# Weight-block sums and sums of squares as accumulating transfers, and one bank copy moved to ScalarE, in a two-layer streaming encoder

## The chip, the cores and the metric

The kernel runs on one core of a Trainium2 chip. The metric is the device time of one execution in microseconds (us); of several runs the median counts. Nothing else runs on the core, and all inputs and outputs lie in device memory.

## What is computed

Two trunk layers work on 656 tokens: 16 meta tokens and 512 prompt tokens of one new stream, and 8 running streams of 16 tokens. Cut to what matters here:

```python
def swiglu(x, w_gate, w_up, w_down):
    return (silu(x @ w_gate) * (x @ w_up)) @ w_down       # 1024 -> 2816 -> 1024

def trunk_layer(x, ...):
    h = x + 0.5 * swiglu(rmsnorm(x, n1), f1g, f1u, f1d)
    ...                                                    # mixers: pooling, short convolution, attention
    h = h + mixed @ w_out
    h = h + 0.5 * swiglu(rmsnorm(h, n2), f2g, f2u, f2d)
```

All data is float32. Four feed-forward networks (FFNs), two per layer, take most of the time.

## The kernel before

Activations lie with channels on the 128 partitions and tokens along the free dimension. Every product splits both operands into a high and a low part and takes three matmuls (`mm3`), so a weight block of 128 channels needs a rounded copy (ScalarE, `act`, L120) and the remainder (VectorE, a subtraction, `tt`, L134) before TensorE can use it. Such a prepared piece of four blocks is a **slab**; raw weights are loaded by the SP queue (L333), and `prep_next` makes slabs of them in order, one after each group of matmuls (`pump`).

The gate and up projections of an FFN work by **pairs** of 128 output columns. A pair is a 2x2 block product done with seven block products instead of eight (`run_pair`): weights a11, a12, a21, a22 (each 128x512, that is 256 KB) become the seven slabs a11, a12, a21', a11', a12', s3, a22, where

- s3 = a11 + a21 (first sum),
- a21' = a21 + a22 (second), a11' = a11 + a21' (third), a12' = a12 + a11' (fourth).

The four sums are made in place by GpSimd in `sums` (L394); each reads what the one before wrote, or overwrites what it read. The raw weights of a pair lie in two tiles A1 (a11, a12) and A2 (a21, a22). There are two sets of such tiles, called raw and rawb in the profile, which pairs use in turn; the s3 buffers (in the tile Wa) are two as well. A set can be loaded again when its last slab is prepared.

TensorE runs a pair as seven groups of 12 matmuls (`seven`, L143) of 128x328 each, into three PSUM banks. In the program's order they are B11, B21, Q1, Q2, B22, T3, and T4, which is held back (`late`) into the next pair. B11, Q2, T3 and T4 add up in one bank b1 (tag mm), so b1 must be read out between two of them: after T3, VectorE reads it (`s[3]` = b1 + p5, L134) before T4 may write.

An FFN has 20 such pairs, 11 column blocks less the first, each with gate and up. Between them stand four groups of eight down-projection units. So the pairs come in runs: 3 at the start, then 6, 6 and 5 in a row, each followed by eight down units. Pairs of a run are written here as g3, u3 (gate and up of column block 3).

The norms need sums of squares over the eight channel blocks. In `feed` (L528) ScalarE squares each block as it is finished, GpSimd adds it to `acc`, and VectorE adds the eighth. This happens ahead of five of the norms, with six additions by GpSimd in each.

The order of instructions on each engine is set once, when the program is built, by a scheduler that goes by priorities and by its own model of durations; each engine then runs its queue strictly in that order, waiting where an operand is late.

Of the kernel before, what the change touches and what calls it, by code (L numbers as in the profile page):

```python
# [7 lines left out]
AF = mybir.ActivationFunctionType  # L8
ALU = mybir.AluOpType

P = 128
# [45 lines left out]
class Builder:  # L57
# [261 lines left out]
    def load_next(self):  # L319
        u = self.units[self.n_load]  # L320
        if self.n_done < u["after"]:
            return False
        spots = self.take("raw", len(u["src"]), u["ring"] == "F")
        if spots is None:
            return False
        u["raw"] = []
        for at, (k, parts) in zip(spots, u["src"]):
            raw = at
            if raw is None:
                raw = self.rp.tile([P, KD * P], F32, tag="raw", name=self.name("raw"))  # L330
            raw = raw.rearrange("p (k c) -> p k c", k=KD)[:, :k, :]
            for k0, kn, src in parts:
                self.nc.sync.dma_start(raw[:, k0:k0 + kn, :], src.rearrange("(k p) c -> p k c", p=P))  # L333
            u["raw"].append((at, raw))
        self.n_load += 1
        return True

# [53 lines left out]
    def sums(self, u, i):  # L391
        if i == 1:
            (_, A1), (_, A2) = u["raw"]
            add = lambda out, a, b: self.nc.gpsimd.tensor_tensor(out, a, b, op=ALU.add)  # L394
            s3 = self.s3[u["turn"]].rearrange("p (k c) -> p k c", k=4)
            a11, a12, a21, a22 = A1[:, 0:4], A1[:, 4:8], A2[:, 0:4], A2[:, 4:8]
            add(s3, a11, a21)
            add(a21, a21, a22)
            add(a11, a21, a11)
            add(a12, a11, a12)  # L400


    def run_units(self, units):
# [104 lines left out]
    def feed(self, to, l, m, hi):  # L508

        c0, c1 = self.halves[hi]  # L510
        gain = {"mixer": "mix_norm", "ffn1": "ffn1_norm", "ffn2": "ffn2_norm"}[to]
        if to == "mixer":
            self.gained(self.H[:, m, c0:c1], l, m, c0, c1, gain)
        if hi == 0:
            return
        c0 = self.halves[0][0]
        n = c1 - c0
        if to != "mixer":
            self.blocks(l, m, gain, c0, n // 2)
        acc, s = self.acc[:, :n], self.sq[self.fed % 2][:, :n]  # L520
        if self.fed == 0:
            self.act(acc, self.H[:, m, c0:c1], AF.Square)
        else:
            self.act(s, self.H[:, m, c0:c1], AF.Square)
            if self.fed == KD - 1:
                self.tt(acc, acc, s, ALU.add)
            else:
                self.nc.gpsimd.tensor_tensor(acc, acc, s, op=ALU.add)  # L528
        self.fed += 1
        if self.fed == KD:  # L530
            self.fed = 0
            halves = self.halves
            self.pending = lambda: self.scales(to, halves)
# [81 lines left out]
    def pair_unit(self, w, f, run, **kw):  # L615

        c = [slice((f + r) * P, (f + r + 1) * P) for r in range(2)]
        self.turn = not self.turn
        return dict(slabs=[4] * 7, src=[(KD, [(0, KD, w[:, x])]) for x in c], prep=self.prep_pair, then=self.sums,
                    run=self.run_pair, evict=run, ring="F", turn=int(self.turn), **kw)  # L620

    def col_unit(self, w, f, r, run):

# [63 lines left out]
    def run_pair(self, u):  # L687

        c0 = self.halves[0][0]
        n = self.halves[0][1] - c0  # L690
        b1, b2, b3 = self.psum("mm"), self.psum("z"), self.psum("z")
        p5 = self.copies[u["turn"]][:, :n]
        f = self.factor[:, c0:c0 + 2 * n]
        S = self.sil if u["evict"] == self.gate_out else self.up
        S = S[:, :4 * n]
        s = [S[:, i * n:(i + 1) * n] for i in range(4)]
        self.clock += 1
        self.seven(u, b1, B11, n, True)
        self.act(s[0], b1[:, :n], AF.Copy)
        self.pump(1)  # L700
        if self.late:
            self.late()
        self.finish_pending()
        self.seven(u, b3, B21, n, True)
        self.tt(s[0], b3[:, :n], s[0], ALU.add)
        self.pump(1)
        self.seven(u, b2, Q1, n, True)
        self.act(p5, b2[:, :n], AF.Copy)
        self.pump(1)
        self.seven(u, b1, Q2, n, False)  # L710
        self.act(s[1], b1[:, :n], AF.Copy)
        self.pump(1)
        self.seven(u, b2, B22, n, False)
        self.tt(s[1], b2[:, :n], s[1], ALU.add)
        self.mul(S[:, :2 * n], S[:, :2 * n], f)
        u["evict"](u, 0, n)
        self.pump(1)
        self.seven(u, b1, T3, n, False)
        self.tt(s[3], b1[:, :n], p5, ALU.add)
        self.stt(s[3], s[3], -1.0, f[:, n:], ALU.mult, ALU.mult)  # L720
        self.pump(1)

        def last():
            self.late = None
            self.seven(u, b1, T4, n, False)
            self.stt(s[2], b1[:, :n], -1.0, f[:, :n], ALU.mult, ALU.mult)
            u["evict"](u, 1, n)
            self.pump(1)
        self.late = last
        self.slot_tail()  # L730
# [507 lines left out]
    def token_scale(self, hi, sums):  # L1238
        c0, c1 = HALF_ALL[hi]
        self.scale_of(sums, c0, c1, False, self.sil, self.up)  # L1240
# [343 lines left out]
```

## Time and profile before

| what | value |
|---|---|
| median of 3 runs (2888.08 to 2892.82) | 2888.17 us |
| the profiled execution's own time | 2890.04 us |
| its span in the profile | 2888.3 us |
| TensorE busy | 2829.0 us, 98% |
| VectorE busy | 1936.6 us, 67% |
| ScalarE busy | 1289.9 us, 45% |
| GpSimd busy | 598.2 us, 21% |
| transfers | 224.27 MB, mean 78 GB/s |

Engines are named PE (TensorE), DVE (VectorE), ACT (ScalarE), POOL (GpSimd) and SP (SyncE, whose queue SPq issues the loads). A row names the line of the helper that recorded an operation, so tile names tell more than lines: ws and slabs are prepared weights, raw and rawb are raw weights, XR and ra hold split activations, mm and z are PSUM banks, Wa is working memory. In a timeline row stand the start, the duration, the engine, the operation, out<-in, and in brackets how long the engine was idle before and what ended that.

### The profile page before, as it was taken

How to read it: one execution, taken by the hardware profiler on the slowest of the kernel's cores; microseconds unless marked ns; L12 is line 12 of the kernel's file. 1: busy time of each engine (PE TensorE's matmuls, PEld its weight loads, DVE VectorE, ACT ScalarE, POOL GpSimd, SP SyncE). 2: the span in 40 equal slices, each digit the busy share in tenths (PEclk: the TensorE clock that was granted, in tenths of full speed). 3: DMA queues.
4: the chain of work that ended last, by engine and by line, in shares of the span. 5: the costliest groups of instructions: out<-in, count | busy, mean ns of one | idle time of the engine just before them, and what ended most of it. 6: DMA issues, size and time to landing. Idle time of an engine off the chain costs nothing.

```text
span 2888.3 us, 47733 instructions
## 1 busy us (share of the span) xinstructions
PE 2829.0 (98%) x19179; PEld 2781.5 (96%) x19179; DVE 1936.6 (67%) x3262; ACT 1289.9 (45%) x2464; POOL 598.2 (21%) x481
## 2 busy tenths in 40 slices
PE   7999999999999999999999999999999999999999
PEld 6999999999999999999999999999999999999999
DVE  8686675876444877675786675768764458675764
ACT  5343344776323443343443443447763234343433
POOL 2233231011000123132223241311110002232230
PEclk8999999999999999999999999999999999999999
DMA  3222322222222322222312322222222223223222
GB/s 113 81 86 69 88 76 74 79 77 69 66 74 74 88 81 66 82 80 74 88 52 81 88 74 81 83 71 72 75 73 66 79 75 88 76 67 92 81 71 76
DMA packets 437169, 224.27 MB, mean 78 GB/s; under 512 B 10110, under 2 KB 436290, under 8 KB 436946
## 3 DMA queue, kind: packets, MB, share of 16 engines
q1 hardware_dynamic: 436452, 220.90, 26.2%
q8 instruction: 150, 2.46, 0.3%
q14 instruction: 73, 0.60, 0.1%
q10 hardware_dynamic: 494, 0.32, 0.0%
HBM read 212.87 MB, written 8.31 MB: 77 GB/s over the span
## 4 chain that ended last, share of the span: by engine, by line
PE 81%; DVE 10%; POOL 4%; DMA 3%; ACT 1%; issue 1%; ACTq 0%; SPq 0%; POOLq 0%; DVEq 0%
PE z L143 50%; PE mm L143 29%; DVE Wa L134 2%; DMA rawb<-in_ffn_w_up_dram 2%; DVE ws L134 2%; DVE Wa L131 2%; DVE slabs L134 2%; POOL rawb L394 1%; POOL raw L394 1%; DVE XR L134 1%; POOL Wa L394 1%; DMA raw<-in_ffn_w_gate_dram 1%; PE aux L143 1%; ACT ws L120 0%; DVE ra L134 0%
## 5 line engine op out<-in xcount | busy, mean ns | idle before, releaser
L143 PE MATMUL mm<-XR,ws 128*128 128x328 f32 (+3 forms) x4848 | 802.6, 314 | 12.6 <-DVE Wa L134 12.6
L143 PEld LDWEIGHTS mm<-XR,ws 128*128 128x128 f32 x4848 | 738.0, 188 | 20.4 <-DVE Wa L134 16.0
L143 PE MATMUL z<-XR,ws 128*128 128x328 f32 (+3 forms) x3924 | 629.2, 313 | 13.5 <-ACT XR L120 6.5
L143 PEld LDWEIGHTS z<-XR,ws 128*128 128x128 f32 x3924 | 597.1, 189 | 15.3 <-ACT XR L120 6.8
L134 DVE TENSOR_TENSOR ws<-raw,ws 128x512 fp32r<-128x512 f32 (+1 forms) x429 | 311.2, 728 | 175.8 <-ACT ws L120 174.0
L143 PE MATMUL z<-ra,ws 128*128 128x328 f32 (+1 forms) x2688 | 421.0, 312 | 0.2
L120 ACT ACTIVATE ws<-raw 128x512 fp32r<-128x512 f32 (+1 forms) x429 | 263.5, 617 | 338.2 <-PE z L143 192.7
L143 PEld LDWEIGHTS z<-ra,ws 128*128 128x128 f32 x2688 | 405.1, 188 | 0.7 <-ACT ra L120 0.4
L143 PE MATMUL z<-ra,slabs 128*128 128x328 f32 (+1 forms) x2112 | 330.9, 312 | 1.8 <-ACT ra L120 1.8
L143 PE MATMUL mm<-XR,slabs 128*128 128x328 f32 (+1 forms) x1944 | 318.9, 312 | 7.9 <-DVE Wa L134 7.7
L143 PEld LDWEIGHTS z<-ra,slabs 128*128 128x128 f32 x2112 | 319.3, 188 | 2.9 <-ACT ra L120 2.4
L143 PEld LDWEIGHTS mm<-XR,slabs 128*128 128x128 f32 x1944 | 296.4, 188 | 10.6 <-DVE Wa L134 9.8
L143 PE MATMUL z<-XR,slabs 128*128 128x328 f32 (+1 forms) x1764 | 296.6, 316 | 9.7 <-DVE Wa L134 6.5
L143 PEld LDWEIGHTS z<-XR,slabs 128*128 128x128 f32 x1764 | 275.1, 192 | 11.2 <-DVE Wa L134 7.0
L131 DVE SCALAR_TENSOR_TENSOR H<-z,H 128x328 f32<-128x328 f32 (+1 forms) x288 | 140.9, 492 | 130.5 <-PE z L143 130.1
L134 DVE TENSOR_TENSOR Wa<-Wa 128x656 f32<-128x656 f32 (+5 forms) x245 | 204.3, 834 | 3.9 <-ACT Wa L120 0.2
L134 DVE TENSOR_TENSOR ws<-rawb,ws 128x512 fp32r<-128x512 f32 (+1 forms) x183 | 147.9, 812 | 83.2 <-ACT ws L120 82.9
L120 ACT ACTIVATE slabs<-raw 128x512 fp32r<-128x512 f32 (+1 forms) x183 | 109.0, 600 | 209.9 <-PE z L143 86.1
L120 ACT ACTIVATE Wa<-Wa 128x656 f32<-128x656 f32 (+7 forms) x232 | 136.9, 597 | 122.6 <-DVE Wa L134 113.6
L134 DVE TENSOR_TENSOR slabs<-raw,slabs 128x512 fp32r<-128x512 f32 (+1 forms) x183 | 145.9, 799 | 61.7 <-ACT slabs L120 61.5
L120 ACT ACTIVATE ws<-rawb 128x512 fp32r<-128x512 f32 (+1 forms) x183 | 108.3, 599 | 172.5 <-PE z L143 94.7
L528 POOL TENSOR_TENSOR Wa<-Wa 128x656 f32<-128x656 f32 (+1 forms) x30 | 55.1, 1837 | 628.7 <-ACT Wa L120 602.5
(177 smaller groups left out, 2943.4 us busy)
## 6 DMA issues: line engine op xcount, KB each, us to landing
raw<-in_w_in_dram SPq DMA_DIRECT2D x88, 512.0 KB, 3.8
raw<-in_ffn_w_gate_dram SPq DMA_DIRECT2D x57, 512.0 KB, 3.7
rawb<-in_ffn_w_up_dram SPq DMA_DIRECT2D x55, 512.0 KB, 4.3
rawb<-in_ffn_w_down_dram SPq DMA_DIRECT2D x48, 384.0 KB, 3.4
raw<-in_ffn_w_down_dram SPq DMA_DIRECT2D x48, 384.0 KB, 3.4
raw<-in_ffn_w_up_dram SPq DMA_DIRECT2D x33, 512.0 KB, 3.7
rawb<-in_ffn_w_gate_dram SPq DMA_DIRECT2D x31, 512.0 KB, 3.8
raw<-in_w_out_dram SPq DMA_DIRECT2D x16, 512.0 KB, 3.9
```

Source lines behind the costliest of these rows:

```text
L120: i = self.nc.scalar.activation(out, in_, func, **kw).ins
L131: return self.nc.vector.scalar_tensor_tensor(out, in0, scalar, in1, op0=op0, op1=op1).ins
L134: self.nc.vector.tensor_tensor(out, in0, in1, op=op)
L143: self.nc.tensor.matmul(out, lhsT, rhs, start=start, stop=stop, skip_group_check=True)
L394: add = lambda out, a, b: self.nc.gpsimd.tensor_tensor(out, a, b, op=ALU.add)
L528: self.nc.gpsimd.tensor_tensor(acc, acc, s, op=ALU.add)
```

## The change

The four sums become four transfers on chip, issued by GpSimd's queue, that add their source to their destination. Since such a transfer only adds to what is there, the first sum needs a11 in the s3 buffer beforehand: a third load per pair, 256 KB from device memory, brings it. The additions of squares by GpSimd become such transfers too. After T3, ScalarE copies b1 into `s[3]` and VectorE adds p5 on chip, so the bank's read is now ScalarE's.

```diff
@@ load_next @@
             u["raw"].append((at, raw))
+        if "turn" in u:
+            self.nc.sync.dma_start(self.s3[u["turn"]].rearrange("p (k c) -> p k c", k=4), u["a11"])
         self.n_load += 1
@@ sums @@
-            add = lambda out, a, b: self.nc.gpsimd.tensor_tensor(out, a, b, op=ALU.add)
             s3 = self.s3[u["turn"]].rearrange("p (k c) -> p k c", k=4)
             a11, a12, a21, a22 = A1[:, 0:4], A1[:, 4:8], A2[:, 0:4], A2[:, 4:8]
-            add(s3, a11, a21)
-            add(a21, a21, a22)
-            add(a11, a21, a11)
-            add(a12, a11, a12)
+            self.grow(s3, a21)
+            self.grow(a21, a22)
+            self.grow(a11, a21)
+            self.grow(a12, a11)
+
+    def grow(self, to, by):
+
+        self.nc.gpsimd.dma_start(to, by, accum_op=ALU.add)
@@ feed @@
-                self.nc.gpsimd.tensor_tensor(acc, acc, s, op=ALU.add)
+                self.grow(acc, s)
@@ pair_unit @@
-                    run=self.run_pair, evict=run, ring="F", turn=int(self.turn), **kw)
+                    run=self.run_pair, evict=run, ring="F", turn=int(self.turn),
+                    a11=w[0:4 * P, c[0]].rearrange("(k p) c -> p k c", p=P), **kw)
@@ run_pair @@
         self.seven(u, b1, T3, n, False)
-        self.tt(s[3], b1[:, :n], p5, ALU.add)
+        self.act(s[3], b1[:, :n], AF.Copy)
+        self.tt(s[3], s[3], p5, ALU.add)
```

The scheduler also gives another order. On GpSimd's queue, in the first run of six pairs (raw_75 and raw_76 are g3's tiles, raw_104 and raw_105 g4's, raw_118 and raw_119 g5's, rawb those of u3 and u4 in turn; Wa is s3), it was, from the end of g3's sums on:

```order
L394 TENSOR_TENSOR raw_75_1027<-raw_75_1027 128x512
L394 TENSOR_TENSOR Wa_86<-raw_104_1374,raw_105_1376 128x512
L394 TENSOR_TENSOR raw_105_1376<-raw_105_1376 128x512
L394 TENSOR_TENSOR rawb_3_105<-rawb_3_105 128x512 x2
L394 TENSOR_TENSOR raw_104_1374<-raw_105_1376,raw_104_1374 128x512
L394 TENSOR_TENSOR Wa_86<-rawb_3_105 128x512
L394 TENSOR_TENSOR rawb_3_105<-rawb_3_105 128x512
L394 TENSOR_TENSOR raw_104_1374<-raw_104_1374 128x512
L394 TENSOR_TENSOR rawb_3_105<-rawb_3_105 128x512 x2
L394 TENSOR_TENSOR Wa_86<-raw_118_1638,raw_119_1640 128x512
```

and it is now, over the same stretch:

```order
L405 DMA raw_75_1034<-raw_75_1034 128x512
L405 DMA Wa_86<-raw_105_1386 128x512
L405 DMA rawb_3_105<-rawb_3_105 128x512
L405 DMA raw_105_1386<-raw_105_1386 128x512
L405 DMA rawb_3_105<-rawb_3_105 128x512
L405 DMA raw_104_1384<-raw_105_1386 128x512
L405 DMA Wa_86<-rawb_3_105 128x512
L405 DMA raw_104_1384<-raw_104_1384 128x512
L405 DMA rawb_3_105<-rawb_3_105 128x512 x2
L405 DMA Wa_86<-raw_119_1654 128x512
L405 DMA rawb_3_105<-rawb_3_105 128x512
```

The sums of two pairs that follow each other now take turns, step by step: u3's third and fourth sum stand on either side of g4's second, and u4's fourth stands behind g5's first.

On ScalarE, from the copy of b1 after Q2 of u3 (mm_108) on, this stood before:

```order
L120 ACTIVATE Wa_86<-mm_108_1480 128x328
L120 ACTIVATE slabs_2_104<-Wa_86 128x512
L120 ACTIVATE slabs_2_104<-raw_104_1374 128x512
L120 ACTIVATE ws_117_1619<-raw_105_1376 128x512
L120 ACTIVATE ws_120_1642<-rawb_3_105 128x512
L120 ACTIVATE ra_41_548<-Wa_86 128x656
L120 ACTIVATE Wa_86<-mm_114_1603 128x328
```

and this stands now:

```order
L120 ACTIVATE Wa_86<-mm_108_1492 128x328
L120 ACTIVATE slabs_2_104<-raw_104_1384 128x512
L120 ACTIVATE slabs_2_104<-Wa_86 128x512
L120 ACTIVATE slabs_2_104<-raw_104_1384 128x512
L120 ACTIVATE ra_41_550<-Wa_86 128x656
L120 ACTIVATE Wa_86<-mm_108_1492 128x328
L120 ACTIVATE ws_117_1633<-raw_105_1386 128x512
L120 ACTIVATE Wa_86<-mm_114_1617 128x328
```

The new copy of b1 (the second row with mm_108, after T3) stands behind the slabs a11', s3 and a12' of g4, and ahead of a22.

## Rows read from the trace of the kernel before

**Rows 1.** The page: busy us of each engine, share of the span
```profile
PE 2829.0 (98%) x19179; PEld 2781.5 (96%) x19179; DVE 1936.6 (67%) x3262; ACT 1289.9 (45%) x2464; POOL 598.2 (21%) x481
```

**Rows 2.** What PE waited for: us in total, times, longest
```profile
PE mm L143 <- DVE Wa L134: 20.3, 19, 1.8
PE z L143 <- DVE Wa L134: 10.1, 3, 3.9
...
PE z L143 <- DVE XR L134: 5.8, 2, 3.3
...
PE z L143 <- DVE slabs L134: 0.6, 2, 0.3
```

**Rows 3.** PE's timeline in the first run of six pairs
```profile
130.30 1.96 PE L143 MATMUL mm<-XR,slabs 128*128 128x328 f32 x12
132.10 3.78 PE L143 MATMUL z<-XR,slabs 128*128 128x328 f32 x24
...
172.10 2.08 PE L143 MATMUL mm<-XR,ws 128*128 128x328 f32 x12 [0.32 <-DVE Wa L134]
```

**Rows 4.** Timeline of all engines just ahead of that wait
```profile
165.30 1.35 DVE L134 TENSOR_TENSOR Wa<-Wa 128x656 f32<-128x656 f32 x1
...
166.58 1.77 DVE L134 TENSOR_TENSOR slabs<-Wa,slabs 128x512 fp32r<-128x512 f32 x1
167.77 1.73 POOL L394 TENSOR_TENSOR raw<-raw 128x512 f32<-128x512 f32 x1
...
169.53 0.63 ACT L120 ACTIVATE slabs<-raw 128x512 fp32r<-128x512 f32 x1 [4.13 <-POOL raw L394]
...
170.19 0.69 DVE L134 TENSOR_TENSOR slabs<-raw,slabs 128x512 fp32r<-128x512 f32 x1 [1.84 <-ACT slabs L120]
...
170.80 0.83 DVE L134 TENSOR_TENSOR Wa<-Wa 128x656 f32<-128x656 f32 x1
...
171.56 0.49 DVE L134 TENSOR_TENSOR Wa<-mm,Wa 128x328 f32<-128x328 f32 x1
```

**Rows 5.** PE's timeline at two FFN starts
```profile
1024.10 7.92 PE L143 MATMUL z<-XR,slabs 128*128 128x328 f32 x51 [2.63 <-DVE Wa L134]
...
1462.51 5.58 PE L143 MATMUL z<-XR,slabs 128*128 128x328 f32 x25 [2.57 <-DVE XR L134]
```

**Rows 6.** POOL's groups: busy us, mean ns, idle before
```profile
L394 POOL TENSOR_TENSOR rawb<-rawb 128x512 f32<-128x512 f32 x90 | 138.3, 1540 | 37.7 <-DVE slabs L134 20.9 <-DVE ws L134 12.7
...
L528 POOL TENSOR_TENSOR Wa<-Wa 128x656 f32<-128x656 f32 x24 | 44.2, 1840 | 383.8 <-ACT Wa L120 357.5 <-DVE H L131 26.2
```

**Rows 7.** DMA issues: KB each, median us from issue to landing
```profile
raw<-in_ffn_w_gate_dram SPq DMA_DIRECT2D x57, 512.0 KB, 3.7
...
rawb<-in_ffn_w_down_dram SPq DMA_DIRECT2D x16, 256.0 KB, 2.8
```

**Rows 8.** SP queue's timeline: one issue; loads of the two tiles of a pair
```profile
92.84 0.37 SPq L333 DMA_DIRECT2D rawb<-in_ffn_w_down_dram  x1
...
139.58 5.71 SPq L333 DMA_DIRECT2D raw<-in_ffn_w_gate_dram  x2
157.99 1.91 SPq L333 DMA_DIRECT2D rawb<-in_ffn_w_up_dram  x2
```

**Rows 9.** POOL's timeline: first sums of g4 and u4, third of g4
```profile
148.78 1.29 POOL L394 TENSOR_TENSOR Wa<-raw,raw 128x512 f32<-128x512 f32 x1 [10.62 <-DMA raw<-in_ffn_w_gate_dram]
...
160.59 1.67 POOL L394 TENSOR_TENSOR raw<-raw,raw 128x512 f32<-128x512 f32 x1 [4.38 <-DVE ws L134]
164.67 1.29 POOL L394 TENSOR_TENSOR Wa<-rawb 128x512 f32<-128x512 f32 x1 [2.41 <-DMA rawb<-in_ffn_w_up_dram]
```

**Rows 10.** Timeline at a norm: two squares on ACT, 128x656
```profile
1450.30 0.75 ACT L120 ACTIVATE Wa<-H 128x656 f32<-128x656 f32 x1
...
1456.67 0.76 ACT L120 ACTIVATE Wa<-H 128x656 f32<-128x656 f32 x1 [1.04 <-DVE H L131]
```

**Rows 11.** ACT's copy of a bank of that size, in a timeline
```profile
164.00 0.42 ACT L120 ACTIVATE Wa<-mm 128x328 f32<-128x328 f32 x1
```

## The prediction

> **What bounds the kernel.** I read the busy times first: TensorE is busy 2829.0 of 2888.3 us [rows 1], so at most 59 us can be won by anything that leaves the matmuls alone. Then I read what TensorE waited for. Its longest total is the wait of bank b1's matmuls for VectorE, 20.3 us in 19 waits; two more kinds of wait for VectorE come to 10.1 and 5.8 us, and for a prepared slab it waits 0.6 us in all [rows 2]. So the weight supply, which the change rebuilds, costs next to nothing now, and VectorE's lateness is what there is to gain. Third, TensorE's timeline: 12 matmuls take 1.80 us (130.30 to 132.10), so a pair of seven groups takes 12.6 us, and T4 of u3 starts late at 172.10 [rows 3]. The timeline of all engines tells why. VectorE's subtraction took 1.77 us while GpSimd added, and 0.69 us when it did not; a multiplication 1.35 against 0.83. Then VectorE stood 1.84 us behind ScalarE, which had waited 4.13 us for GpSimd's sum; only at 171.56 did it read b1 [rows 4]. Eighteen of the 19 waits lie in the FFNs, which I put at 18.5 us (the other is in the mixer, 1.8).
>
> **The bank's copy.** 80 copies of 0.42 us [rows 11] go to ScalarE, 34 us on an engine busy 45% of the span [rows 1]. VectorE keeps 80 additions; nothing is saved there. b1 is now free when ScalarE has read it. In the new order that copy stands behind the slab a12' of the next pair and behind the split of u's product, so it waits for the fourth sum. Before, ScalarE began that slab at 169.53 [rows 4]; if the fourth sum is no later, the copy ends at 169.53 + 0.63 + 0.75 (the split, as long as the 128x656 steps of [rows 10]) + 0.42 = 171.3 instead of 172.05, and T4 does not wait. Ends for this edit: all 18.5 us, or nothing if the copy is always as late as VectorE's read was. I take two thirds, **-12 us**, since in the case worked out the lead is 0.7 us against waits of about 1 us.
>
> **GpSimd's adds go.** 320 sums of about 1.5 us (90 of them are 1540 ns in the mean) and 30 of 1.84 us leave GpSimd [rows 6]. Their time was cheap, but VectorE was slowed beside them. At FFN starts TensorE waits for VectorE's chain of splits and scales: 2.63 and 2.57 us in two cases [rows 5], 12.6 us over four, which are the 10.1 of the second kind and one of the third [rows 2]. Between none and all of this can go; I take a third, **-4 us**, because most of such a chain is made of VectorE's own steps.
>
> **The sums as transfers.** No row shows an accumulating transfer, so its length L, from issue to the sum's being usable, has to be bounded. It moves 256 KB but reads source and destination. The nearest rows are the load of 256 KB, 2.8 us, and that of 512 KB, 3.7 us [rows 7]; the second has as many bytes to read. The low end is 2.8. The high end is two 512 KB loads one after another, 7.4, for a queue that GpSimd has to serve and an addition in the path. I take 3.7 and 0.4 for the issue (0.37 on the SP queue [rows 8]), **L = 4.1 us**, nearest to the 512 KB row.
>
> The Trainium skill, page "DMA: Bandwidth & Descriptors", section "Anatomy of one DMA — SWDGE (gpsimd) path", gives a GpSimd-issued transfer about 2.0 us fixed plus its bytes at 436 GB/s, which is an estimate of 2.6 us for 256 KB, below my low end. By it four sums take 10.4 us, the copies are never held, and the sum of this prediction would be -22.5 us. No run here shows such a transfer yet, and the page's figure is for plain copies.
>
> What does the chain of four bear? It is serial: each sum reads or overwrites the one before. A set of raw tiles serves every second pair, so its loop must fit into 2 x 12.6 = 25.2 us. The loop is: load A2 to first sum, 3.9 us in one case (issued at 139.58 + 5.71 - 0.37 = 144.9, first sum at 148.78) and 5.2 in the next (159.5 to 164.67) [rows 8, 9], so 4.5; four sums, 4L; and the slabs a12', s3 and a22 after them, two ScalarE steps of 0.63 and one each of 0.63 and 0.69 [rows 4], 2.6. So 7.1 + 4L <= 25.2, or **L <= 4.5 us**. Before, with 1.5 us sums, this was 13 us, and slabs were held back by full buffers. At 4.1 the loop is 23.5 us: it fits, barely.
>
> I also followed the first run by hand with the new order. g4's first sum starts at 148.78 [rows 9] and lands at 152.9; its second lands at 157. Its third waits for slab a11 to be read, as it did before (160.59, [rows 9]), and lands at 164.7; the fourth lands at 169.3, where it ended at 169.50 before [rows 4]. So the slab that ScalarE waited for is ready at the same moment, since the second sum's lateness is hidden behind the wait for slab a11. TensorE needs it after T4 of u3, which began at 172.10 [rows 3] and lasts 1.8. Queued behind a waiting sum on GpSimd is the other pair's next sum, which the new order puts there; on ScalarE, behind a late slab, bank copies, at 1 to 2 us of slack. For that I add **+1 us** over the program.
>
> **What costs nothing while it is covered.** The third load is 80 x 256 KB; A2, freed last, is the load that the first sum waits for. Where the new load is issued behind A2's, 0.4 us is added to the loop above. The squares: one comes every 6.4 us (1450.30 to 1456.67 [rows 10]), and a transfer of 336 KB at about 4.6 us fits in. Without that cover each us above 6.4 is paid six times at five norms, 30 us.
>
> **Sum.** -12 - 4 + 1 = -15 us against the profiled execution's 2890.0, so 2875. That execution lies 1.9 us above the median of the runs, so for the median I say 2888.2 - 15 = **2873 us**. The forecast's own range is 2857 (all of 18.5 + 12.6 gone) to 2882 (half of the T4 waits remain and the starts gain nothing). A measurement of this kernel can tell about 0.2%, 5.8 us, from no change.
>
> **Rivals.**
>
> *A, the transfers are too long.* Beyond L = 4.5 each pair that reloads its tiles within a run loses half the loop's excess, 2(L - 4.5) us. In the runs of 6, 6 and 5 that is all but the first two: 4 + 4 + 3 = 11 per FFN, 44 in all. At L = 5 this is +44 us, at 5.5 +88, at 6 +132. With the -15 the balance turns at L = 4.67; 5.5 gives 2961, 6 gives 3005, and the high end 7.4 gives 3128. TensorE would then wait for slabs, and ScalarE for sums. For it: the margin up to 4.5 is 0.4 us, L is unmeasured, and a sum must travel through GpSimd's queue and read its destination. Against it: the 512 KB row, and the reserve of slabs prepared ahead after each stretch of down units. Chance 0.32; slower.
>
> *B, the wait changes its engine only.* ScalarE's copy of b1 sits behind the slab that waits for the fourth sum; with L between 4.3 and 4.6 it is as late as VectorE's read was, and the 12 us stay. Then -4 + 1 gives 2885. For it: the new order of ScalarE. Against it: the worked case, where the fourth sum ends at the same time. Chance 0.10; no change.
>
> *C, VectorE is not relieved.* Its slow steps might come from transfers or ScalarE and not from GpSimd, or the new transfers slow it as much. Then only the copy's part, -12 + 2, is left: 2878. Against it: 0.69 and 1.77 us for the same subtraction, without and with an add beside it [rows 4]. Chance 0.06; faster.
>
> **How the numbers follow.** The forecast has 0.52, so faster by over 0.2% is 0.58 with C, no change 0.10 (B), slower 0.32 (A). The range must leave out at most 0.2: its low end is 2857, and its high end reaches into A to L = 5.5, 2961, above which I leave about 0.15.
>
> **What would show it.** Right: GpSimd's busy time falls by some 540 us (320 x 1.54 and 30 x 1.84) to under 70; subtractions at about 0.69 us in the mean in FFNs; T4's waits for VectorE under 6 us in all; transfers on GpSimd's queue landing 3.5 to 4.5 us after issue; slab waits of TensorE under 5 us. Wrong: landings over 4.8 us, TensorE waiting for slabs by tens of us in the fourth and fifth pair of a run, or ScalarE named before T4 as often as VectorE was.

## The result, and the profile after

The changed kernel takes **2912.70 us** (median of 4 runs, 2906.84 to 2913.48); the kernel before, run beside it, 2888.93 us (median of 4). The ratio is 1.0075, with a 95% interval of 1.0058 to 1.0093: slower by 0.75%, where 2873 us, 0.5% faster, was forecast. The profiled execution took 2913.48 us, its span is 23.4 us longer than before.

The page's busy times, which answer to [rows 1]:

```profile
PE 2839.0 (98%) x19179; PEld 2783.1 (96%) x19179; DVE 1744.7 (60%) x3262; ACT 1306.6 (45%) x2544; POOL 361.2 (12%) x481
```

VectorE lost 192 us of work and GpSimd 237, and yet the kernel is slower: neither was the bound. What TensorE waited for (us in total, times, longest), answering to [rows 2]:

```profile
PE mm L143 <- ACT Wa L120: 40.7, 41, 3.2
...
PE mm L143 <- DVE Wa L131: 6.2, 4, 2.3
...
PE mm L143 <- DVE Wa L134: 1.8, 1, 1.8
...
PE z L143 <- DVE XR L134: 0.8, 1, 0.8
PE z L143 <- DVE ws L134: 0.4, 1, 0.4
```

The waits that the change was forecast to shorten are gone: of the first kind only the mixer's 1.8 us are left of 20.3, of the two kinds at FFN starts 0.8 of 15.9. Prepared slabs are not late either (0.4). A new kind stands in their place: TensorE waits 41 times, 40.7 us, for ScalarE's copies of PSUM banks; before there was one such wait, of 0.2 us. All waits of the list come to 68.1 us against 54.5, which is 13.6 of the 23.4; TensorE's own busy time is 10.0 longer, to which the last section returns.

The starts of the same matmul in both traces say where. At the program's start and the later FFN starts the new kernel gains 3.1, 2.9, 9.8 and 6.8 us, 22.6 in all; in the mixers and down units next to nothing moves; in the runs of pairs it loses some 46 us.

The timeline of all engines in the first run of six, the place of [rows 4]:

```profile
161.52 0.68 DVE L134 TENSOR_TENSOR ws<-raw,ws 128x512 fp32r<-128x512 f32 x1
...
162.60 0.86 POOL L405 DMA_DIRECT2D raw<-raw  x1 [5.98 <-DVE Wa L131]
...
164.50 0.86 POOL L405 DMA_DIRECT2D Wa<-rawb  x1 [1.04 <-DMA rawb<-in_ffn_w_up_dram]
166.64 0.63 ACT L120 ACTIVATE slabs<-raw 128x512 fp32r<-128x512 f32 x1 [2.92 <-DMA raw<-raw]
...
167.25 0.84 POOL L405 DMA_DIRECT2D raw<-raw  x1 [1.89 <-DMA raw<-raw]
...
172.39 0.63 ACT L120 ACTIVATE slabs<-raw 128x512 fp32r<-128x512 f32 x1 [4.60 <-DMA raw<-raw]
172.93 0.73 ACT L120 ACTIVATE ra<-Wa 128x656 fp32r<-128x656 f32 x1
...
173.57 0.42 ACT L120 ACTIVATE Wa<-mm 128x328 f32<-128x328 f32 x1
...
174.05 2.06 PE L143 MATMUL mm<-XR,ws 128*128 128x328 f32 x12 [2.25 <-ACT Wa L120]
```

Read it from the end. T4 of u3 waited 2.25 us for the copy of b1, a step of 0.42 us on an engine that is idle 55% of the span. The copy stood third in ScalarE's queue, behind slab a12' of g4, and ScalarE had waited 4.60 us for that slab's sum. The third sum of g4, which had to wait until VectorE had read slab a11 (161.52 to 162.20), was issued at 162.60 and usable at 166.64 (4.0 us later), the fourth issued at 167.25 and usable at 172.39 (5.1). (The first POOL row names L131, an instruction of VectorE that ended at 162.60 too; what the sum waits for is the read of a11.)

ScalarE's waits for sums, the three largest of eight kinds:

```profile
ACT slabs L120 <- DMA raw<-raw: 61.3, 26, 4.6
ACT slabs L120 <- DMA rawb<-rawb: 55.0, 20, 8.6
ACT ws L120 <- DMA rawb<-rawb: 54.6, 24, 5.5
```

The eight come to 338.8 us; before, the four kinds of wait for GpSimd's sums came to 161.6. Going back from each of TensorE's waits for a bank copy to the last idle time of ScalarE, 32 of them, 34.0 us, lead to a slab that waited for a transfer.

DMA issues (KB each, median us to landing), answering to [rows 7]:

```profile
raw<-in_ffn_w_gate_dram SPq DMA_DIRECT2D x57, 512.0 KB, 4.6
...
raw<-raw POOLq DMA_DIRECT2D x90, 256.0 KB, 3.3
rawb<-rawb POOLq DMA_DIRECT2D x90, 256.0 KB, 3.3
...
Wa<-Wa POOLq DMA_DIRECT2D x24, 328.0 KB, 4.1
```

### The profile page after: what moved, and what is told of

Its sections match the earlier page's. It is cut to its first block, busy times and chain, and to the rows that moved or that the text cites. A ratio compares the mean times of both kernels' runs of the same rounds, so it can differ in the third digit from the quotient of the medians.

```text
span 2911.7 us, 48524 instructions
## 1 busy us (share of the span) xinstructions
PE 2839.0 (98%) x19179; PEld 2783.1 (96%) x19179; DVE 1744.7 (60%) x3262; ACT 1306.6 (45%) x2544; POOL 361.2 (12%) x481
## 5 line engine op out<-in xcount | busy, mean ns | idle before, releaser
L134 DVE TENSOR_TENSOR ws<-raw,ws 128x512 fp32r<-128x512 f32 (+1 forms) x429 | 287.8, 673 | 234.8 <-ACT ws L120 233.7
L134 DVE TENSOR_TENSOR Wa<-Wa 128x328 f32<-128x328 f32 (+5 forms) x325 | 214.8, 668 | 16.2 <-ACT Wa L120 12.4
L131 DVE SCALAR_TENSOR_TENSOR H<-z,H 128x328 f32<-128x328 f32 (+1 forms) x288 | 139.7, 493 | 132.9 <-PE z L143 132.7
L134 DVE TENSOR_TENSOR ws<-rawb,ws 128x512 fp32r<-128x512 f32 (+1 forms) x183 | 118.8, 652 | 139.2 <-ACT ws L120 139.0
L120 ACT ACTIVATE slabs<-rawb 128x512 fp32r<-128x512 f32 (+1 forms) x181 | 107.8, 599 | 208.7 <-PE z L143 91.0
L134 DVE TENSOR_TENSOR slabs<-rawb,slabs 128x512 fp32r<-128x512 f32 (+1 forms) x181 | 117.5, 651 | 136.1 <-ACT slabs L120 135.6
L134 DVE TENSOR_TENSOR slabs<-raw,slabs 128x512 fp32r<-128x512 f32 (+1 forms) x183 | 119.0, 652 | 128.7 <-ACT slabs L120 128.3
```

Source lines behind the costliest of these rows:

```text
L120: i = self.nc.scalar.activation(out, in_, func, **kw).ins
L131: return self.nc.vector.scalar_tensor_tensor(out, in0, scalar, in1, op0=op0, op1=op1).ins
L134: self.nc.vector.tensor_tensor(out, in0, in1, op=op)
```

## Experiments

Three theories at first. **H**: the bank copies stand in ScalarE's order behind slabs whose sums, as transfers, land later than GpSimd's did. **T**: the traffic itself costs (loads of 512 KB of gate weights take 4.6 us instead of 3.7). **K**: moving the read of b1 to ScalarE is what costs. Each edit also gets its own order from the scheduler, so two runs differ by an edit and an order together. Ratios are to the kernel before, on the same chip.

| run | us | ratio, 95% interval |
|---|---|---|
| e1_squares | 2888.34 | 0.9996 [0.9986, 1.0005] |
| e2_copy | 2876.12 | 0.9960 [0.9945, 0.9975] |
| e3_sums | 2912.23 | 1.0078 [1.0063, 1.0093] |
| e4_sums_squares | 2905.97 | 1.0069 [1.0048, 1.0089] |
| e5_late_wait | 2840.75 | 0.9829 [0.9814, 0.9844] |
| k1_chain3 | 2945.94 | 1.0199 [1.0179, 1.0218] |
| h4_half | 2844.38 | 0.9841 [0.9826, 0.9855] |
| h3_one | 2855.14 | 0.9879 [0.9864, 0.9894] |
| e6_late_two | 2918.21 | 1.0096 [1.0081, 1.0112] |
| e8_bank_first | 2903.50 | 1.0040 [1.0027, 1.0053] |
| h2_half_copy | 2858.81 | 0.9885 [0.9870, 0.9900] |
| h1_half | 2868.45 | 0.9926 [0.9909, 0.9942] |
| e10_turns | 2981.01 | 1.0307 [1.0287, 1.0326] |
| e9_k1_turns | 2878.93 | 0.9963 [0.9950, 0.9976] |

### The change's parts, one at a time

The kernel before with the squares alone as transfers:

```diff
-                self.nc.gpsimd.tensor_tensor(acc, acc, s, op=ALU.add)
+                self.nc.gpsimd.dma_start(acc, s, accum_op=ALU.add)
```

> Only the sums of squares are transfers; weight sums stay GpSimd's additions and VectorE reads b1 after T3. Theory H (ScalarE's bank copies stand behind slabs that wait for transferred sums; the norms gain because VectorE is no longer slowed): no weight sum is a transfer, so no loss in the runs of pairs; the 22.7 us that the change won at the starts of FFNs come in part, 5 to 12 us: 2877 to 2884 us. Rival K (the moved bank copy is what costs): the same 2877 to 2884, since the copy isn't moved. Rival T (the added traffic slows the loads): 94 MB of transfers become 10 MB, so at most a few us either way, 2884 to 2891.

2888.34 us, no change, where H had expected a part of the gain (2877 to 2884). Of the two kinds of wait for VectorE at FFN starts the first is still there (10.2 us); of the second 2.5 us have gone (3.3 of 5.8 are left). So most of that gain is not the squares'.

The kernel before with the bank's copy alone:

```diff
-        self.tt(s[3], b1[:, :n], p5, ALU.add)
+        self.act(s[3], b1[:, :n], AF.Copy)
+        self.tt(s[3], s[3], p5, ALU.add)
```

> Only the read of b1 after T3 is moved to ScalarE; all sums stay GpSimd's additions. H: ScalarE waits for GpSimd's sums no longer than before (162 us in all), so TensorE's waits for VectorE before T4 (18.5 us) go in good part and little comes in their place: 2874 to 2884 us. K: ScalarE's queue is late by itself, TensorE waits for it about as often as in the change (41 us in 41 waits): 2900 to 2915 us. T: as before without the T4 waits, 2874 to 2884.

2876.12 us, 12.9 less than before: the prediction's -12. What TensorE waited for in this run:

```profile
PE z L143 <- DVE Wa L134: 9.8, 3, 4.4
...
PE mm L143 <- ACT Wa L120: 4.5, 8, 1.3
PE mm L143 <- DVE Wa L131: 4.4, 5, 1.4
...
PE mm L143 <- DVE Wa L134: 1.8, 1, 1.8
```

The waits ahead of T4 are gone, and few come back for ScalarE, so K has it wrong: the moved copy by itself gains.

The weight sums and the third load alone (the parts of the change in `load_next`, `sums`, `grow` and `pair_unit`):

> Only the weight sums are transfers (with the third load); squares are GpSimd's additions and VectorE reads b1 after T3. H: ScalarE still waits some 340 us for sums and its copies after B11 and Q2 are late, and VectorE's read of b1 stands behind slabs of the same kind: 2905 to 2925 us, with TensorE's waits split between ScalarE and VectorE. K: no moved copy, so no loss and part of the gain at the norms: 2870 to 2885 us. T: the loss of the change stays, with TensorE waiting for slabs, not for bank copies: 2905 to 2920.

2912.23 us: the whole loss. TensorE's waits:

```profile
PE mm L143 <- DVE Wa L134: 18.0, 16, 3.0
PE mm L143 <- ACT Wa L120: 17.6, 16, 2.2
```

The loss is there without the moved copy, which is against K too. Of VectorE's waits at FFN starts the 10.1 us are gone and 3.0 of the 5.8 are left, so it was for the most part the weight sums leaving GpSimd that relieved VectorE.

The change with VectorE still reading b1 (e3 and e1 together):

> The change without the moved copy: weight sums and squares are transfers, VectorE reads b1 after T3. H: within 8 us of the change, 2905 to 2920 us, since two of the three copies from b1 were ScalarE's before and VectorE waits for ScalarE's slabs. K: the loss goes, the norms' gain stays: 2863 to 2875 us. T: 2905 to 2920, with loads landing as late as in the change (4.6 us for 512 KB of the gate weights against 3.7).

2905.97 us. The copy, worth -12.9 us with GpSimd's sums, is worth nothing with transfers: the medians differ by +6.7 us (2912.70 less 2905.97), but the ratios to the kernel before, 1.0075 and 1.0069, not beyond their intervals. VectorE's waits ahead of T4 turn into ScalarE's: here TensorE waits 17.7 us for VectorE and 19.1 for ScalarE's copies, with the change 1.8 and 40.7. Three bank copies of a pair (after B11, Q1 and Q2) were ScalarE's already, and they wait in the same way.

### The same traffic, with the waiting slab last

```diff
             self.grow(s3, a21)
-            self.grow(a21, a22)
-            self.grow(a11, a21)
-            self.grow(a12, a11)
+            self.grow(a22, a21)
+            self.grow(a22, a21)
+            self.grow(a22, a21)
```

> The change with as many transfers of the same size in the same chain, but the second, third and fourth sums are all added onto the block a22, so that a21', a11' and a12' are read unsummed and only the last slab, a22, waits for them (the second to fourth sums are left out of the computation and put on a22). Theory H (bank copies on ScalarE stand in its order behind slabs that wait for a chain of four transfers): TensorE's waits for ScalarE's copies fall from 40.7 us to under 12, time 2850 to 2890 us. Theory T (the loss is the transfers' traffic: weight loads take 4.6 us instead of 3.7, and everything on chip shares the transfer engines): the traffic is the same, so 2900 to 2917 us.

2840.75 us, below the range of either theory. (This kernel leaves out the second to fourth sums of a21', a11' and a12', so it serves for its time alone.) Of the 40.7 us there is left:

```profile
PE mm L143 <- ACT Wa L120: 0.2, 1, 0.2
```

The traffic is all there (339.21 MB, loads of 512 KB of gate and up weights from 4.2 to 4.9 us), the loss is not. T falls: bytes cost nothing that shows. What costs is which slab waits, or how late: here no sum has to wait for the read of slab a11, and g4's fourth transfer is issued at 155.23 instead of 167.25, so this run changes both at once.

### Which of the sums costs

If the length of the chain is what counts, one link less must help. With a21 loaded into s3 and a11 added, the second sum need not wait for the first:

```diff
-            self.grow(s3, a21)
+            self.grow(s3, a11)
...
-                    a11=w[0:4 * P, c[0]].rearrange("(k p) c -> p k c", p=P), **kw)
+                    a11=w[0:4 * P, c[1]].rearrange("(k p) c -> p k c", p=P), **kw)
```

> The change with one edit that leaves count and size of the transfers as they are: the third load brings a21 instead of a11, and the first sum adds a11 to it, so that the second sum, which overwrites a21, does not have to wait until the first has read it: the chain is three transfers long instead of four. H: every third and fourth sum lands about 3.5 to 4 us earlier, TensorE's waits for ScalarE's copies fall from 40.7 us to under 22, time 2870 to 2897 us. T: as the change, 2904 to 2917 us.

2945.94 us, slower by 33 us than the change: a miss against both theories, taken up below.

On top of it, GpSimd's additions again for the third and fourth sum:

```diff
-            self.grow(a11, a21)
-            self.grow(a12, a11)
+            self.nc.gpsimd.tensor_tensor(a11, a21, a11, op=ALU.add)
+            self.nc.gpsimd.tensor_tensor(a12, a11, a12, op=ALU.add)
```

> As the run with a chain of three, but the third and fourth sums are GpSimd's additions again: the first two sums are transfers beside each other. H: the chain is one transfer (3.5 us) and 1.5 + 1.8 us of additions, about as long as GpSimd's four additions before (6.5 us); TensorE's waits for ScalarE's copies under 12 us, time 2855 to 2878 us. T: half of the transfers of weights, so about half of the loss against the run with the copy alone (2876 us): 2885 to 2897 us.

2844.38 us, **faster than both kernels** by 1.6% and more, and below H's range as well (2855 to 2878). GpSimd's timeline, g4's third and fourth sum at 161.50 and 163.78:

```profile
160.88 0.86 POOL L405 DMA_DIRECT2D Wa<-rawb  x1 [7.86 <-DMA Wa<-in_ffn_w_up_dram]
161.50 1.56 POOL L400 TENSOR_TENSOR raw<-raw,raw 128x512 f32<-128x512 f32 x1
162.88 1.03 POOL L405 DMA_DIRECT2D rawb<-rawb  x1
163.78 1.83 POOL L401 TENSOR_TENSOR raw<-raw 128x512 f32<-128x512 f32 x1
```

The fourth sum ends at 165.6, where the change had it at 172.4, and TensorE waits 1.3 us for bank copies in the whole program.

With the second sum GpSimd's too, so that only s3 is a transfer:

```diff
-            self.grow(a21, a22)
+            self.nc.gpsimd.tensor_tensor(a21, a21, a22, op=ALU.add)
```

> Only the sum s3 is a transfer (third load of a21, a11 added to it); the other three sums are GpSimd's additions, the squares transfers, the third bank's copy ScalarE's. H: the chain is three additions (4.9 us), no transfer in it, shorter than before; TensorE's waits for ScalarE's copies under 8 us, time 2862 to 2878 us, between, as GpSimd's additions stay beside VectorE at the FFN starts for the most part. T: a quarter of the transfers of weights, 2880 to 2888 us.

2855.14 us, better than either theory said. So the count of transfers is not the measure: none costs 2876 (e2_copy), one 2855, two early ones 2844. This gave a sharper theory, **H2**: the third sum overwrites a11 and must wait until that slab has been prepared, late in the pair; only what comes after that point counts. The complement tests it, the change with the first and second sum as additions and the third and fourth as transfers:

```diff
-            self.grow(s3, a21)
-            self.grow(a21, a22)
+            self.nc.gpsimd.tensor_tensor(s3, a11, a21, op=ALU.add)
+            self.nc.gpsimd.tensor_tensor(a21, a21, a22, op=ALU.add)
```

> The change with the first and second sums done by GpSimd's additions again, the third and fourth as transfers: the complement of h4_half. Theory H2 (only the third and fourth sums matter: the third can't start before slab a11 has been read, and two transfers then stand between that and slab a12'; the first and second have slack): TensorE's waits for ScalarE's copies stay over 28 us, time 2898 to 2920 us. Theory H1 (each transfer in the chain costs alike): about half of the loss against h4_half, 2870 to 2890 us.

2918.21 us, with

```profile
PE mm L143 <- ACT Wa L120: 41.1, 34, 3.3
```

With half of the transfers the whole loss is there, 74 us above h4_half. Not all of the 74 is the copies' doing. TensorE's waits for them are 39.8 us longer than in h4_half, and its busy time is 21.4 longer. The rest is at the FFN starts, where the waits for VectorE are back: 14.4 us (9.5 of them in the row below) against 1.2 in h4_half.

```profile
PE z L143 <- DVE Wa L134: 9.5, 3, 4.2
```

So, as far as these two runs show, it was GpSimd's first two sums that held up VectorE at the FFN starts; where GpSimd does the last two (h4_half), hardly any of these waits are left. From the issue of the third sum to the usable fourth it takes 3.6 us before and about 7.8 after the change (median of 80 pairs each).

Two more with late sums by GpSimd. The first is h4_half without k1's edit:

> The change with the third and fourth sums done by GpSimd's additions (as h4_half, but the third load and the first sum as in the change, so that the second sum waits for the first). H2: the early transfers have slack, so as h4_half: 2840 to 2860 us. H1: one transfer more in the chain than h4_half, 2855 to 2880 us.

2858.81 us, where both readings overlap (H2 up to 2860, H1, by which every transfer in the chain costs alike, from 2855), so it does not decide between them. It is 14 us above h4_half: the early sums' slack is not without bounds. Against e6_late_two, with as many transfers, it is 59 us faster, 33 of them waits for the copies, and that is what speaks for H2. And with VectorE reading b1:

> As h2_half_copy, but the third bank of a pair is read by VectorE as before the change. If the copy on ScalarE is worth as much with short late sums as it was with GpSimd's sums (12.8 us): 10 to 16 us above h2_half_copy, with 15 to 20 us of TensorE's waits for VectorE's subtraction ahead of the seventh product. If VectorE, relieved of GpSimd's additions, is no longer late: within 4 us of h2_half_copy.

2868.45 us, 9.6 more, with 17.6 us in which b1's matmuls waited for VectorE: between what the two readings said, nearer to the first. With the late sums done by GpSimd the copy is again worth most of what e2_copy showed.

### The order of the queues

Must the copies stand behind those slabs? One rule for ScalarE, by an ordering without a wait:

```diff
-        self.act(ws[:, 0], src, AF.Copy)
+        copy = self.act(ws[:, 0], src, AF.Copy)
+        if "then" in u and 2 <= i <= 5 and self.lastc:
+            self.after(copy, self.lastc)
...
-        self.act(s[0], b1[:, :n], AF.Copy)
+        self.lastc = self.act(s[0], b1[:, :n], AF.Copy)
```

(so for all four copies of a pair.)

> The change with one rule for ScalarE's order and nothing else: the slabs a21', a11', a12' and s3 may not stand ahead of a bank's copy that is written before them in the program. Sums, transfers and copies are the same. If the loss is the copies' place behind waiting slabs: TensorE's waits for ScalarE's copies fall from 40.7 us to under 22, time 2865 to 2897 us. If it isn't (the slabs themselves are late, or the place in the order doesn't matter): 2903 to 2920 us, with waits for slabs or VectorE's subtractions in their place.

2903.50 us, 9 less than the change, the waits for the copies 38.4 us in 37: a miss for H. The time lies at the edge of the second reading's range, but the waits for slabs or VectorE that it named did not come. It does not say that the place is harmless: slabs are prepared some groups ahead, so that the program itself writes them ahead of copies that TensorE needs sooner, and the rule leaves those where they are. 25 waits, 25.8 us, still lead to a slab that waited for a transfer.

Then k1's riddle. Its GpSimd timeline around g4's sums:

```profile
149.72 0.87 POOL L405 DMA_DIRECT2D raw<-raw  x1 [1.72 <-DVE ws L134]
150.41 1.05 POOL L405 DMA_DIRECT2D rawb<-rawb  x1
...
162.70 0.87 POOL L405 DMA_DIRECT2D rawb<-rawb  x1 [0.58 <-DMA rawb<-in_ffn_w_up_dram]
165.30 0.84 POOL L405 DMA_DIRECT2D Wa<-rawb  x1 [1.74 <-DMA rawb<-in_ffn_w_up_dram]
166.54 0.86 POOL L405 DMA_DIRECT2D raw<-raw  x1 [0.40 <-issue]
```

g4's fourth sum (166.54) stands behind both early sums of u4, which wait for their loads, and u3's third (150.41) behind g4's second. The scheduler had moved them there. So a rule for GpSimd: a pair's four sums are all issued before the next pair's first.

```diff
-            self.grow(s3, a21)
-            self.grow(a21, a22)
+            first = [self.grow(s3, a21), self.grow(a21, a22)]
+            for i in first:
+                if self.fourth:
+                    self.after(i, self.fourth)
             self.grow(a11, a21)
-            self.grow(a12, a11)
+            self.fourth = self.grow(a12, a11)
...
-        self.nc.gpsimd.dma_start(to, by, accum_op=ALU.add)
+        return self.nc.gpsimd.dma_start(to, by, accum_op=ALU.add).ins
```

On the change:

> The change with one rule for GpSimd's order: the first two sums of a pair are issued after the fourth sum of the pair ahead. If a good part of the lateness is the queue (a third or fourth sum stands behind the next pair's first sum, which waits for its load): TensorE's waits for ScalarE's copies fall from 40.7 us to under 25, time 2870 to 2900 us. If it is the two transfers behind the read of slab a11: within 8 us of the change, 2905 to 2921 us, or slower, as the next pair's first sums now come later.

On k1_chain3:

> The run with a chain of three (2945.9 us) under the same rule for GpSimd's order. If its 33 us above the change came from fourth sums behind two load-waiting sums of the next pair: 2880 to 2912 us, no slower than the change. If from elsewhere (ScalarE's order, where 42 copies instead of 32 stand behind a waiting slab): 2925 us or more.

2981.01 and 2878.93 us: the rule costs the change 68 us, far beyond the "or slower" that was allowed for, and gives k1 67, a shade more than the first reading said. GpSimd's timeline of e10_turns, g4's four sums:

```profile
157.22 0.84 POOL L407 DMA_DIRECT2D Wa<-raw  x1
162.12 0.85 POOL L407 DMA_DIRECT2D raw<-raw  x1 [4.06 <-DMA Wa<-raw]
168.31 0.86 POOL L407 DMA_DIRECT2D raw<-raw  x1 [5.33 <-DMA raw<-raw]
172.15 0.86 POOL L407 DMA_DIRECT2D raw<-raw  x1 [2.98 <-DMA raw<-raw]
```

and of e9_k1_turns:

```profile
150.81 0.84 POOL L407 DMA_DIRECT2D Wa<-raw  x1
151.36 1.19 POOL L407 DMA_DIRECT2D raw<-raw  x1
158.18 0.86 POOL L407 DMA_DIRECT2D raw<-raw  x1 [5.64 <-DMA raw<-raw]
163.33 0.87 POOL L407 DMA_DIRECT2D raw<-raw  x1 [4.28 <-DMA raw<-raw]
```

In turns, the early sums come after the pair ahead, so the whole chain is laid bare: four transfers in a row, 14.9 us from first to fourth issue, or two side by side and two in a row, 12.5. The two programs differ by the link that k1 takes out, and by whatever the scheduler made of it; together that is 102 us. In e10_turns TensorE also waits for slabs, some 30 us in all, where it does so for under 2 us in every other run; the largest kind:

```profile
PE mm L143 <- DVE slabs L134: 19.2, 7, 5.1
```

So k1's edit is right and its loss was the queue's order, as far as the rule moved nothing but that; the scheduler may have answered to it elsewhere. Why the scheduler chose k1's order stays open, and the copies' rule and GpSimd's were not tried together.

## Why the prediction was wrong

**The bank's copy, -12.** Right by itself (-12.9 alone), worth nothing in the change. The step that failed is its premise, "if the fourth sum is no later", and the hand-walk that it stood on: "lands at 164.7; the fourth lands at 169.3". By its own L of 4.1 the fourth would land at 168.8; the walk does not say what its other 0.5 us are. The third sum was issued at 162.60 instead of 160.6, since slab a11 was read 1.7 us later (161.52 in the rows of the result, against this one of the kernel before) and the issue came 0.4 us after that:

```profile
159.84 0.68 DVE L134 TENSOR_TENSOR ws<-raw,ws 128x512 fp32r<-128x512 f32 x1
```

From the third's landing to the fourth's issue it took 0.6 us, and the fourth took 5.1 us instead of 4.1. So 172.39, and the copy was 2.3 us late instead of 0.7 early. Beyond that one case, the walk took one pair for 80.

**Copies behind late slabs, +1.** This is the term that was mis-sized: the mechanism stands in the prediction ("on ScalarE, behind a late slab, bank copies, at 1 to 2 us of slack"), but it was given 1 us and measured 40.5 us more of waits for ScalarE's copies. The walk looked at T4 alone; each of a pair's four reads by ScalarE can stand there. In sum, the runs of pairs lost 46 us where the forecast had them gain 11.

**The length L.** 350 transfers took a median of 3.5 us from issue to landing, at least 3.14, one in ten over 4.8, the longest 6.9; those of 256 KB have medians from 3.3 to 3.9, by the tiles between which they run. The 4.1 lies above the median, and yet the chain was too slow, because the third and fourth come where TensorE's need is near: they start only after the read of a11, and two of them take about 7.8 us. The Trainium skill's estimate of 2.6 us (page "DMA: Bandwidth & Descriptors", section "Anatomy of one DMA — SWDGE (gpsimd) path", which does not say whether its fit holds for transfers that add) is below all 350; that the copies would never be held, as the prediction worked out from it, the 40.7 us refute.

**The loop of the raw tiles, and rival A.** The median landing stayed under 4.5, and slab waits at 0.4 us: right, and rival A did not happen in the change. In e10_turns, where the chain of g4 stands bare, a link took 5.0 us in the mean (14.9 for three), above the 4.5, and there TensorE did wait some 30 us for slabs, as rival A has it. The reason for slower was another: the loop asks whether four sums fit into two pairs, while what counted was how long two of them take after the read of a11.

**Rival B** named the place, ScalarE's copy behind the slab with the fourth sum, but let it do no worse than VectorE had done, 2885 us. It did. (The forecast range's 2882 does not come out of its own terms either: half of 18.5 gone and 1 added gives 2880.)

**GpSimd's adds go, -4.** Under-sized: the two kinds of wait fell from 15.9 to 0.8 us, and the starts gained 22.6. Most of what lies between is the clock: before, it was granted at 1.2 instead of 2.4 GHz from 1463.0 to 1466.4, 1483.5 to 1486.9 and 2452.9 to 2459.7 us, about waits of 2.6, 3.6 and 3.9 us, and after the change it stays at 2.4 GHz there. Half of these 13.6 us is 6.8. 128x512 subtractions fell to where they ran undisturbed in [rows 4]:

```profile
L134 DVE TENSOR_TENSOR slabs<-raw,slabs 128x512 fp32r<-128x512 f32 (+1 forms) x183 | 119.0, 652 | 128.7 <-ACT slabs L120 128.3
```

(652 ns in the mean, 799 before, with 24 half-size ones among them.) Rival C fell.

**The squares at nothing** held in the time (e1_squares). GpSimd's busy time fell to 361 us, not under 70, as the issue of a transfer takes GpSimd 0.86 us; nobody waited for that.

## What to carry to other kernels

Before a sum moves to a transfer, find what it has to wait for and who reads it next: in this kernel a sum whose operands lie ready long ahead can take 3.5 us, one that waits for a late read cannot, and the fastest complete version here (h4_half) uses transfers for the first two sums and GpSimd for the last two. A late operand costs what stands behind its reader in the in-order queue, not what the reader itself is needed for: list for each short step on the path what can stand in front of it. And a hand-walk through one pair, with a margin of 0.7 us, is no proof for 80.

## What the runs showed of the hardware

- Issuing an accumulating transfer occupies GpSimd for 0.86 us, 350 times about the same, while the SP queue's issues take 0.37 us [rows 8].
- An accumulating transfer on chip of 256 KB takes 3.1 to 3.2 us when no other transfer runs beside it, and up to 6.0 with loads beside it; the 6.9 was one of 320 KB. With them, the median load of 512 KB for gate weights went from 3.7 us [rows 7] to 4.6, without a loss that shows (e5_late_wait).
- TensorE's busy time, for the same matmuls, goes with its waits: 2816.6 us in e5_late_wait, 2818.4 in h4_half, 2829.0 before, 2839.0 after, 2863.4 in e10_turns. The traces say where it is booked. At the full clock a matmul takes 146 ns up to the next one's start, but 304 to 306 ahead of a wait and 240 to 246 behind one (before and after the change; the ends of matmuls are modelled in the profile). A wait so brings some 0.25 us of busy time with it. The change has 65 waits of over 50 ns, the kernel before 39: some 7 of the 10.0 us.
- The granted clock moves with the waits too. After the change it fell to 1.2 GHz in the runs of pairs at 1402.2, 2576.4, 2596.9 and 2839.2 us, each time about a wait of 1.9 to 2.4 us and for 3.4 us, where the kernel before kept 2.4 GHz. Over the whole program it comes out alike, 0.994 against 0.993 of full speed in the mean; in e10_turns it is 0.986, with 84 us at 1.2 GHz against 38 before.
